# Layer 1 of a two-layer decoder trunk: output projection and feed-forward with one 512-column product per weight block

## The chip, the core and the metric

The kernel runs on one core of one Trainium2 chip. A core has TensorE (matrix products out of SBUF into PSUM banks of 512 fp32 columns; the trace calls its products PE and its weight loads PEld), VectorE (DVE), ScalarE (ACT), GpSimd (POOL) and SyncE (SP, which here issues nearly all DMAs). The metric is the device time of one execution in microseconds; the median of several runs is compared.

## What is computed

Two layers run over 272 tokens (16 meta tokens and 256 real ones) of width 1024. The part that the change touches is, per layer:

```python
merged = (gates[:, :, 0] * (out_a @ wb_a.T) + gates[:, :, 1] * (out_b @ wb_b.T)
          + gates[:, :, 2] * (out_c @ wb_c.T))
h_res = h_res + merged @ w_out[layer]
h2 = _rmsnorm(h_res, ln2_g[layer])
h_res = h_res + jnp.square(jax.nn.relu(h2 @ w_ff1[layer])) @ w_ff2[layer]
```

`w_out` is 1024x1024, `w_ff1` 1024x4096, `w_ff2` 4096x1024. Ahead of it in each layer stand one wide input projection and three attention branches. The meta tokens are dropped at the end, so layer 1 computes its queries, its output projection and its feed-forward for 256 tokens only, where layer 0 does so for all 272.

## The kernel before, in words

Activations lie transposed: features on the 128 partitions, tokens along the free dimension. `T` is 272; `q0` is 0 in layer 0 and 16 in layer 1, and `NQ = T - q0` is 272 and 256. All weights come from one packed array `wall`, in 2048-column DMAs into three `raw` buffers.

**Split precision.** Every large product is made of three fp32r matmuls. `split` (line 171) takes an fp32 tile apart: ScalarE casts it to fp32r (line 172, the high part `H`), VectorE subtracts that from the source (line 173, the low part `L`). `ws.next` does so with each weight block of 128x1024 (tiles `wh` and `wl`, three buffers each). `mm3` (lines 175 to 180) then issues three matmuls into one PSUM bank: weight high by activation high (line 178), weight low by activation high (line 179), weight high by activation low (line 180). Each loads its own 128x128 of weights and streams 272 or 256 columns of activations. The three together, for one 128x128 block of a weight, are called a block below.

**Stages of layer 1 that matter here.** *Output projection* (`wo`): 8 output tiles of 8 blocks each, from the merged branches in `mg`; the first two tiles run as a pair, interleaved, into banks of `ps_t`. `wo_done` adds the bank to the residual `xT` (line 982) and feeds the tile to the next norm: `NormIn.feed` makes its high and low part (lines 279 and 280) and the sum of squares (lines 293 and 294). *First feed-forward product* (`ff1`): 32 tiles of 8 blocks; the first two as a pair again, and right behind them the matmul of the norm's sum (line 300). `ff1_done` evicts: ScalarE's ReLU from PSUM to SBUF (line 1015), VectorE's square (line 1017), and a split into the pairs `fHL`, or `fH` and `fL`. *Second feed-forward product* (`ff2`): 8 tiles of 32 blocks; VectorE multiplies the bank by the squared norm factor (line 1038), adds it to `xT` (line 1039), and in layer 1 SyncE sends the tile out (line 1041). Apart from the two pairs, these stages use the pool `ps_acc` of two banks: a tile's bank is written again two tiles later, once it has been evicted. In all that makes 64 + 256 + 256 = 576 blocks, 72 times eight of them, and 1728 matmuls in layer 1.

**Order.** The order of the instructions on each engine is fixed when the program is built, by a scheduler that sorts ready instructions by their place in the program; each engine then works its queue strictly in that order, waiting on semaphores. In these stages the cast of a weight block waits until the tile that used its buffer three blocks earlier is finished.

**Other users of 512 columns.** `mla_prep` of each layer multiplies the latent by `ukv` in products of 512 columns (tiles `ps_uk` and `ps_vm`), with a weight load each; in the trace they are the only fp32r products of that width.

Of the kernel before, what the change touches and what calls it, by code (L numbers as in the profile page):

```python
# [79 lines left out]
def hybrid_trunk_kernel(ctx: ExitStack, tc: tile.TileContext, xin, wall, pcol, prow, consts, out):  # L80
# [100 lines left out]

    def minus_sums(ps, srcs):
# [82 lines left out]
    class NormIn:  # L265


        def __init__(self, l, gcol, off):
            self.l, self.g, self.off = l, gcol, off
            self.H = xg_p.tile([P, KD, T], F32R, tag="xgH", name="xgH")  # L270
            self.L = xg_p.tile([P, KD, T], F32R, tag="xgL", name="xgL")
# [35 lines left out]
    def gemm(w, h, c0, m=P, bank=0):  # L307

        pool, tag = ((ps_acc, "acc"), (ps_s, "s"), (ps_t, "t"))[bank]
        ps = pool.tile([P, 512], F32, tag=tag, name="acc")  # L310
        for kc in range(KD):
            mm3(ps[:m, : T - c0], blocks(w, kc, m), (h.H[:, kc, c0:], h.L[:, kc, c0:]), kc == 0, kc == KD - 1)
        return ps

    def proj(h, name, idx, c0, m=P, bank=0):
        return gemm(ws.next(name, idx), h, c0, m, bank)

    def gemm_pair(wl, h, c0):
        pss = s_banks(2)
        for kc in range(KD):  # L320
            for w, ps in zip(wl, pss):
                mm3(ps[:, : T - c0], blocks(w, kc), (h.H[:, kc, c0:], h.L[:, kc, c0:]), kc == 0, kc == KD - 1)
# [13 lines left out]
    def proj_group(h, names, c0s, banks):  # L336
        wl = [ws.next(n, i) for n, i in names]
        pss = banks(len(names))
        for kc in range(KD):
            for w, ps, c0 in zip(wl, pss, c0s):  # L340
                mm3(ps[:, : T - c0], blocks(w, kc), (h.H[:, kc, c0:], h.L[:, kc, c0:]), kc == 0, kc == KD - 1)
# [20 lines left out]
    def layer(l, h, rows):  # L362
# [591 lines left out]
        mg = [(v4(big("mgH", F32R)), v4(big("mgL", F32R))) for _ in range(2)]  # L954
        for j in range(KD):
# [17 lines left out]
            split(mg[j // 4][0][:, j % 4, :NQ], mg[j // 4][1][:, j % 4, :NQ], m[:, :NQ])  # L973
# [4 lines left out]
        def wo_rhs(k):  # L978
            return mg[k // 4][0][:, k % 4, :NQ], mg[k // 4][1][:, k % 4, :NQ]

        def wo_done(j, ps):
            V.tensor_tensor(out=xT[:, j, q0:], in0=xT[:, j, q0:], in1=ps[:, :NQ], op=ALU.add)
# [4 lines left out]
        for k in range(KD):  # L987
            for w, ps in zip(wl, pss):
                mm3(ps[:, :NQ], blocks(w, k), wo_rhs(k), k == 0, k == KD - 1)
        for j in range(2):  # L990
            wo_done(j, pss[j])
        for j in range(2, KD):
            w = ws.next("wo", j)
            ps = ps_acc.tile([P, 512], F32, tag="acc", name="acc")
            for k in range(KD):
                mm3(ps[:, :NQ], blocks(w, k), wo_rhs(k), k == 0, k == KD - 1)
# [5 lines left out]
        def act_pair(i):  # L1002

            g, r = divmod(i, 4)
            if g not in acts:
                if g < 3:
                    t = huge("fHL", F32R)
                    acts[g] = (v4(t), v4(t[:, 4 * T :]))
                else:
                    acts[g] = (v4(big("fH", F32R)), v4(big("fL", F32R)))  # L1010
            return acts[g][0][:, r, :NQ], acts[g][1][:, r, :NQ]

        def ff1_done(i, ps):
            r = row_p.tile([P, T], F32, tag="row", name="ffr")
            S.activation(r[:, :NQ], ps[:, :NQ], AF.Relu)  # L1015
            s = row_p.tile([P, T], F32, tag="row", name="ffs")
            V.tensor_tensor(out=s[:, :NQ], in0=r[:, :NQ], in1=r[:, :NQ], op=ALU.mult)  # L1017
# [175 lines left out]
```

## Time and profile before

| | |
|---|---|
| median of 3 runs | 977.07 us (976.43 to 977.22) |
| the profiled execution | 977.4 us |
| its span, from the first to the last instruction | 975.6 us |
| TensorE busy | 964.4 us (99%), 7614 matmuls |
| weight loads busy | 926.5 us (95%) |
| VectorE busy | 654.2 us (67%) |
| ScalarE busy | 588.7 us (60%) |
| granted TensorE clock | 1.000 |
| HBM read | 147.04 MB, 152 GB/s over the span |

Matmuls overlap in the records (a 256-column matmul's row is 0.28 us long, while the next one starts 0.12 us after it), so what TensorE really spends on one is read from start to start, not from the duration or the busy share. The granted clock of 1.000 is the upper of the two levels, 2.4 GHz. Some matmul records are missing, so counts out of the trace are a few below those of the program.

### The profile page before, as it was taken

What the parts mean: (1) busy time and instruction counts of PE and PEld (TensorE: products, weight loads), DVE (VectorE), ACT (ScalarE), POOL (GpSimd) and SP (SyncE); (2) the same over time, 40 slices, a digit from 0 to 9 for tenths busy, and PEclk for the clock granted to TensorE, in tenths of its full rate; (3) what the DMA queues carried; (4) which work ended last, traced back from release to release, by engine and by line L of the source; (5) the groups of instructions that cost most, each with busy time, mean ns of one, the idle gap of its engine ahead of it and who ended that gap; (6) DMA issues with size and microseconds to landing.
All of it is one profiled execution on the core that took longest, in us unless ns stands there. A gap on an engine that the chain in (4) does not pass through costs nothing.

```text
span 975.6 us, 18642 instructions
## 1 busy us (share of the span) xinstructions
PE 964.4 (99%) x7614; PEld 926.5 (95%) x7614; DVE 654.2 (67%) x1313; ACT 588.7 (60%) x1168; POOL 1.9 (0%) x7
## 2 busy tenths in 40 slices
PE   8999999999999999999999999999999999999998
PEld 7999999889999999999999998989899999999998
DVE  6975457686787666655557754487778876775553
ACT  6776777778635555544436777766795465554332
POOL 0000000000000000000000000000000000000000
PEclk9999999999999999999999999999999999999999
DMA  8432222325454445554544322324345555555551
GB/s 295 168 131 87 88 87 87 130 87 174 162 206 166 162 178 176 176 179 175 178 157 163 130 88 89 128 87 141 134 152 199 178 204 183 178 190 201 184 198 46
DMA packets 23958, 149.28 MB, mean 153 GB/s; under 512 B 2801, under 2 KB 4337, under 8 KB 8257
## 3 DMA queue, kind: packets, MB, share of 16 engines
q1 hardware_dynamic: 23760, 147.77, 43.6%
q8 instruction: 60, 0.98, 0.4%
q0 software_dynamic: 112, 0.33, 0.1%
q14 instruction: 26, 0.20, 0.1%
HBM read 147.04 MB, written 1.05 MB: 152 GB/s over the span
## 4 chain that ended last, share of the span: by engine, by line
PE 91%; DVE 4%; ACT 3%; DMA 1%; issue 0%; SPq 0%; DVEq 0%
PE acc L178 24%; PE acc L180 24%; PE acc L179 24%; PE ps_s L601 2%; PE accs L180 2%; PE accs L178 2%; PE accs L179 2%; PE ps_qkT L672 1%; ACT wh L172 1%; DVE wl L173 1%; PE ps_p L632 1%; PE ps_z L760 1%; PE acct L179 1%; PE acct L178 1%; PE acct L180 1%; PE pv_m L654 1%
## 5 line engine op out<-in xcount | busy, mean ns | idle before, releaser
L173 DVE TENSOR_TENSOR wl<-rawt,wh 128x1024 fp32r<-128x1024 f32 (+1 forms) x273 | 327.9, 1203 | 153.8 <-ACT wh L172 152.9
L172 ACT CAST wh<-rawt 128x1024 fp32r<-128x1024 f32 (+1 forms) x273 | 280.4, 1029 | 201.2 <-PE acc L180 177.2
L178 PE MATMUL acc<-xgH,wh 128*128 128x272 f32 (+2 forms) x1280 | 371.7, 290 | 1.0 <-DVE gate L892 0.9
L179 PE MATMUL acc<-xgH,wl 128*128 128x272 f32 (+2 forms) x1280 | 367.8, 287 | 1.2 <-DVE wl L173 1.2
L180 PE MATMUL acc<-xgL,wh 128*128 128x272 f32 (+2 forms) x1280 | 367.5, 287 | 0.0
L178 PEld LDWEIGHTS acc<-xgH,wh 128*128 128x128 f32 (+1 forms) x1280 | 240.0, 188 | 3.9 <-DVE gate L892 1.7
L179 PEld LDWEIGHTS acc<-xgH,wl 128*128 128x128 f32 (+1 forms) x1280 | 239.7, 187 | 2.9 <-DVE wl L173 1.7
L180 PEld LDWEIGHTS acc<-xgL,wh 128*128 128x128 f32 (+1 forms) x1280 | 240.0, 188 | 1.7 <-issue 1.3
L180 PE MATMUL acc<-fL,wh 128*128 128x272 f32 (+1 forms) x320 | 91.3, 285 | 0.0
L179 PE MATMUL acc<-fH,wl 128*128 128x272 f32 (+1 forms) x320 | 91.1, 285 | 0.0
L178 PE MATMUL acc<-fH,wh 128*128 128x272 f32 (+1 forms) x320 | 91.1, 285 | 0.0
L1015 ACT ACTIVATE ffr<-acc 128x272 f32<-128x272 f32 (+1 forms) x60 | 23.5, 391 | 73.5 <-PE acc L180 73.5
L180 PEld LDWEIGHTS acc<-fL,wh 128*128 128x128 f32 x320 | 60.4, 189 | 0.0
L178 PEld LDWEIGHTS acc<-fH,wh 128*128 128x128 f32 x320 | 60.4, 189 | 0.0
L179 PEld LDWEIGHTS acc<-fH,wl 128*128 128x128 f32 x320 | 60.2, 188 | 0.0
L180 PE MATMUL acc<-fHL,wh 128*128 128x272 f32 (+1 forms) x192 | 54.8, 285 | 0.0
L178 PE MATMUL acc<-fHL,wh 128*128 128x272 f32 (+1 forms) x192 | 54.7, 285 | 0.0
L179 PE MATMUL acc<-fHL,wl 128*128 128x272 f32 (+1 forms) x192 | 54.7, 285 | 0.0
L1017 DVE TENSOR_TENSOR ffs<-ffr 128x272 f32<-128x272 f32 (+1 forms) x64 | 27.8, 434 | 28.6 <-ACT ffr L1015 28.5
L180 PEld LDWEIGHTS acc<-fHL,wh 128*128 128x128 f32 x192 | 36.2, 189 | 0.0
L178 PEld LDWEIGHTS acc<-fHL,wh 128*128 128x128 f32 x192 | 36.2, 189 | 0.0
L179 PEld LDWEIGHTS acc<-fHL,wl 128*128 128x128 f32 x192 | 36.1, 188 | 0.0
(304 smaller groups left out, 1602.3 us busy)
## 6 DMA issues: line engine op xcount, KB each, us to landing
rawt<-wall SPq DMA_DIRECT2D x122, 1024.0 KB, 4.9
rawt<-wall SPq DMA_DIRECT2D x12, 768.0 KB, 4.2
rawt<-wall SPq DMA_DIRECT2D x4, 896.0 KB, 4.8
rawt<-wall SPq DMA_DIRECT2D x6, 256.0 KB, 7.1
xT<-xin SPq DMA_DIRECT2D x4, 272.0 KB, 6.7
rawt<-wall SPq DMA_DIRECT2D x2, 512.0 KB, 6.3
out<-xT SPq DMA_DIRECT2D x8, 128.0 KB, 3.9
rawt<-wall SPq DMA_DIRECT2D x1, 640.0 KB, 3.8
```

What stands on the lines that cost most here:

```text
L172: S.copy(dH, src)
L173: V.tensor_tensor(out=dL, in0=src, in1=f(dH), op=ALU.subtract)
L178: PE.matmul(ps, lhsT=aH, rhs=bH, start=start, stop=False)
L179: PE.matmul(ps, lhsT=aL, rhs=bH, start=False, stop=False)
L180: PE.matmul(ps, lhsT=aH, rhs=bL, start=False, stop=stop)
L601: PE.matmul(ps[:, po : po + nk], lhsT=qa[:, qo - q0 : qo - q0 + P], rhs=ka[:, k0 : k0 + nk], start=True, stop=True)
L632: PE.transpose(p1[:, P * i : P * i + P], a, ident)
L654: PE.matmul(pv[:, o : o + n], lhsT=vs[w], rhs=pt[:, 256 * w : 256 * w + n], start=False, stop=w == 1)
L672: PE.transpose(ps[:96, o : o + n], src[c][:n, hd, :], ident[:n, :n])
L760: PE.matmul(z[:, :W], lhsT=upper, rhs=s[:, :W], stop=False, **kw)
L1015: S.activation(r[:, :NQ], ps[:, :NQ], AF.Relu)
L1017: V.tensor_tensor(out=s[:, :NQ], in0=r[:, :NQ], in1=r[:, :NQ], op=ALU.mult)
```

## The change

In layer 1 (`NQ == SEQ`) the products of `wo`, `ff1` and `ff2` take a new form. The high and the low part of an activation now lie side by side in one tile (`xgHL`, `mgHL`, `fHL`: for each feature block first the high and then the low columns, 272 apart). One matmul multiplies the weight's high part by both, as one moving operand of two runs of 256 columns, into 512 columns of a bank; a second multiplies the weight's low part by the activation's high part into the first 256. So a bank holds two halves, and whoever evicts it sums them: `joined` copies the second half to SBUF (ScalarE) and adds the first (VectorE). `ff1_done` calls it in place of the ReLU, and does ReLU and square in one VectorE instruction; the eviction of `ff2` calls it ahead of its multiplication; `wo_done` adds both halves to `xT`, one after the other. Layer 0, and all products ahead of `wo` in layer 1, keep their three matmuls; for them only the layout of the tiles changes.

```diff
--- before.py
+++ after.py
@@ -179,6 +179,25 @@
         PE.matmul(ps, lhsT=aL, rhs=bH, start=False, stop=False)
         PE.matmul(ps, lhsT=aH, rhs=bL, start=False, stop=stop)
 
+    def dense(ps, a, HL, start, stop, side=False):
+
+
+        aH, aL = a
+        n = HL.shape[2]
+        if not side:
+            mm3(ps[:, :n], a, (HL[:, 0], HL[:, 1]), start, stop)
+        else:
+            PE.matmul(ps[:, : 2 * n], lhsT=aH, rhs=HL, start=start, stop=False)
+            PE.matmul(ps[:, :n], lhsT=aL, rhs=HL[:, 0], start=False, stop=stop)
+
+    def joined(out, ps, n):
+
+        if n > SEQ:
+            return ps[:, :n]
+        S.copy(out, ps[:, n : 2 * n])
+        V.tensor_tensor(out=out, in0=out, in1=ps[:, :n], op=ALU.add)
+        return out
+
     def minus_sums(ps, srcs):
 
         for i, src in enumerate(srcs):
@@ -267,8 +286,8 @@
 
         def __init__(self, l, gcol, off):
             self.l, self.g, self.off = l, gcol, off
-            self.H = xg_p.tile([P, KD, T], F32R, tag="xgH", name="xgH")
-            self.L = xg_p.tile([P, KD, T], F32R, tag="xgL", name="xgL")
+            self.HL = xg_p.tile([P, KD, 2, T], F32R, tag="xgHL", name="xgHL")
+            self.H, self.L = self.HL[:, :, 0], self.HL[:, :, 1]
             self.ss = st_p.tile([P, T], F32, tag="ss", name="ss", bufs=1)
             self.n = 0
 
@@ -304,22 +323,22 @@
     def blocks(w, kc, m=P):
         return w[0][:, kc * m : kc * m + m], w[1][:, kc * m : kc * m + m]
 
-    def gemm(w, h, c0, m=P, bank=0):
+    def gemm(w, h, c0, m=P, bank=0, side=False):
 
         pool, tag = ((ps_acc, "acc"), (ps_s, "s"), (ps_t, "t"))[bank]
         ps = pool.tile([P, 512], F32, tag=tag, name="acc")
         for kc in range(KD):
-            mm3(ps[:m, : T - c0], blocks(w, kc, m), (h.H[:, kc, c0:], h.L[:, kc, c0:]), kc == 0, kc == KD - 1)
+            dense(ps[:m], blocks(w, kc, m), h.HL[:, kc, :, c0:], kc == 0, kc == KD - 1, side)
         return ps
 
-    def proj(h, name, idx, c0, m=P, bank=0):
-        return gemm(ws.next(name, idx), h, c0, m, bank)
+    def proj(h, name, idx, c0, m=P, bank=0, side=False):
+        return gemm(ws.next(name, idx), h, c0, m, bank, side)
 
     def gemm_pair(wl, h, c0):
         pss = s_banks(2)
         for kc in range(KD):
             for w, ps in zip(wl, pss):
-                mm3(ps[:, : T - c0], blocks(w, kc), (h.H[:, kc, c0:], h.L[:, kc, c0:]), kc == 0, kc == KD - 1)
+                dense(ps, blocks(w, kc), h.HL[:, kc, :, c0:], kc == 0, kc == KD - 1)
         return pss
 
     def spread_bank(i):
@@ -333,12 +352,12 @@
     def s_banks(n):
         return [ps_s.tile([P, 512], F32, tag="s", name="accs") for _ in range(n)]
 
-    def proj_group(h, names, c0s, banks):
+    def proj_group(h, names, c0s, banks, side=False):
         wl = [ws.next(n, i) for n, i in names]
         pss = banks(len(names))
         for kc in range(KD):
             for w, ps, c0 in zip(wl, pss, c0s):
-                mm3(ps[:, : T - c0], blocks(w, kc), (h.H[:, kc, c0:], h.L[:, kc, c0:]), kc == 0, kc == KD - 1)
+                dense(ps, blocks(w, kc), h.HL[:, kc, :, c0:], kc == 0, kc == KD - 1, side)
         return pss
 
     def big(name, dt=F32):
@@ -951,7 +970,7 @@
                     tc.add_manual_dep(i, u.name, NOSYNC, reason="table order")
                 sig.append(i)
 
-        mg = [(v4(big("mgH", F32R)), v4(big("mgL", F32R))) for _ in range(2)]
+        mg = [big("mgHL", F32R).rearrange("p (a i t) -> p a i t", a=2, i=2) for _ in range(4)]
         for j in range(KD):
             wab = ws.next("wbab", j)
             sigmoids(j)
@@ -970,30 +989,31 @@
                     t = row_p.tile([P, T], F32, tag="row", name="mrt")
                     V.tensor_tensor(out=t[:, :NQ], in0=ps[:, :NQ], in1=g, op=ALU.mult)
                     V.tensor_tensor(out=m[:, :NQ], in0=m[:, :NQ], in1=t[:, :NQ], op=ALU.add)
-            split(mg[j // 4][0][:, j % 4, :NQ], mg[j // 4][1][:, j % 4, :NQ], m[:, :NQ])
+            split(mg[j // 2][:, j % 2, 0, :NQ], mg[j // 2][:, j % 2, 1, :NQ], m[:, :NQ])
 
         load_log_exp(sig)
         n2 = NormIn(l, PC_LN2, q0)
 
         def wo_rhs(k):
-            return mg[k // 4][0][:, k % 4, :NQ], mg[k // 4][1][:, k % 4, :NQ]
+            return mg[k // 2][:, k % 2, :, :NQ]
 
         def wo_done(j, ps):
-            V.tensor_tensor(out=xT[:, j, q0:], in0=xT[:, j, q0:], in1=ps[:, :NQ], op=ALU.add)
+            for a in (0, NQ)[: 2 if NQ == SEQ else 1]:
+                V.tensor_tensor(out=xT[:, j, q0:], in0=xT[:, j, q0:], in1=ps[:, a : a + NQ], op=ALU.add)
             n2.feed(j)
 
         wl = [ws.next("wo", j) for j in range(2)]
         pss = t_banks(2)
         for k in range(KD):
             for w, ps in zip(wl, pss):
-                mm3(ps[:, :NQ], blocks(w, k), wo_rhs(k), k == 0, k == KD - 1)
+                dense(ps, blocks(w, k), wo_rhs(k), k == 0, k == KD - 1, NQ == SEQ)
         for j in range(2):
             wo_done(j, pss[j])
         for j in range(2, KD):
             w = ws.next("wo", j)
             ps = ps_acc.tile([P, 512], F32, tag="acc", name="acc")
             for k in range(KD):
-                mm3(ps[:, :NQ], blocks(w, k), wo_rhs(k), k == 0, k == KD - 1)
+                dense(ps, blocks(w, k), wo_rhs(k), k == 0, k == KD - 1, NQ == SEQ)
             wo_done(j, ps)
 
 
@@ -1001,30 +1021,37 @@
 
         def act_pair(i):
 
-            g, r = divmod(i, 4)
+            g, r = divmod(i, 2)
             if g not in acts:
-                if g < 3:
-                    t = huge("fHL", F32R)
-                    acts[g] = (v4(t), v4(t[:, 4 * T :]))
+                if i < 12:
+                    t = huge("fHL", F32R)[:, : 8 * T].rearrange("p (g a i t) -> p g a i t", g=2, a=2, i=2)
+                    acts[g], acts[g + 1] = t[:, 0], t[:, 1]
                 else:
-                    acts[g] = (v4(big("fH", F32R)), v4(big("fL", F32R)))
-            return acts[g][0][:, r, :NQ], acts[g][1][:, r, :NQ]
+                    acts[g] = big("fHL", F32R).rearrange("p (a i t) -> p a i t", a=2, i=2)
+            return acts[g][:, r, :, :NQ]
 
         def ff1_done(i, ps):
             r = row_p.tile([P, T], F32, tag="row", name="ffr")
-            S.activation(r[:, :NQ], ps[:, :NQ], AF.Relu)
             s = row_p.tile([P, T], F32, tag="row", name="ffs")
-            V.tensor_tensor(out=s[:, :NQ], in0=r[:, :NQ], in1=r[:, :NQ], op=ALU.mult)
-            split(*act_pair(i), s[:, :NQ])
-
-        pss = proj_group(n2, [("ff1", i) for i in range(2)], [q0] * 2, t_banks)
+            if NQ > SEQ:
+                S.activation(r[:, :NQ], ps[:, :NQ], AF.Relu)
+                V.tensor_tensor(out=s[:, :NQ], in0=r[:, :NQ], in1=r[:, :NQ], op=ALU.mult)
+            else:
+                joined(r[:, :NQ], ps, NQ)
+                V.scalar_tensor_tensor(
+                    out=s[:, :NQ], in0=r[:, :NQ], scalar=0.0, in1=r[:, :NQ], op0=ALU.max, op1=ALU.mult
+                )
+            t = act_pair(i)
+            split(t[:, 0], t[:, 1], s[:, :NQ])
+
+        pss = proj_group(n2, [("ff1", i) for i in range(2)], [q0] * 2, t_banks, NQ == SEQ)
         for i in range(2):
             ff1_done(i, pss[i])
         n2.finish()
         r2 = n2.rstd
         S.activation(r2[:, q0:], r2[:, q0:], AF.Square)
         for i in range(2, 32):
-            ff1_done(i, proj(n2, "ff1", i, q0))
+            ff1_done(i, proj(n2, "ff1", i, q0, side=NQ == SEQ))
 
         nxt = None if last else NormIn(l + 1, PC_LN1, 0)
         for j in range(KD):
@@ -1033,9 +1060,9 @@
                 w = ws.next("ff2", 4 * j + i)
                 for k in range(8):
                     kk = 8 * i + k
-                    mm3(ps[:, :NQ], blocks(w, k), act_pair(kk), kk == 0, kk == 31)
+                    dense(ps, blocks(w, k), act_pair(kk), kk == 0, kk == 31, NQ == SEQ)
             t = row_p.tile([P, T], F32, tag="row", name="fft")
-            V.tensor_tensor(out=t[:, :NQ], in0=ps[:, :NQ], in1=r2[:, q0:], op=ALU.mult)
+            V.tensor_tensor(out=t[:, :NQ], in0=joined(t[:, :NQ], ps, NQ), in1=r2[:, q0:], op=ALU.mult)
             V.tensor_tensor(out=xT[:, j, q0:], in0=xT[:, j, q0:], in1=t[:, :NQ], op=ALU.add)
             if last:
                 nc.sync.dma_start(out[j], xT[:, j, q0:])
```

## Rows read from the trace of the kernel before

**Rows 1.** The page: TensorE's busy time, its granted clock, and the chain's lines

```profile
PE 964.4 (99%) x7614; PEld 926.5 (95%) x7614; DVE 654.2 (67%) x1313; ACT 588.7 (60%) x1168; POOL 1.9 (0%) x7
...
PEclk9999999999999999999999999999999999999999
...
PE 91%; DVE 4%; ACT 3%; DMA 1%; issue 0%; SPq 0%; DVEq 0%
```

**Rows 2.** Stretches, TensorE alone: length, busy (matmuls), granted clock, DMA share, GB/s

```profile
772.60:795.20 22.60, 22.60 (x194) 1.00 0.53 187
795.20:881.30 86.10, 86.10 (x729) 1.00 0.52 184
881.30:972.00 90.70, 90.65 (x767) 1.00 0.47 162
```

**Rows 3.** Waits from 770 us on: waiting for: total us, times, longest

```profile
DVE wl L173 <- ACT wh L172: 54.2, 65, 1.6
ACT wh L172 <- PE acc L180: 53.2, 31, 1.8
ACT ffr L1015 <- PE acc L180: 34.4, 29, 1.3
```

**Rows 4.** Timeline of ScalarE in ff1: start, us, instruction [idle before <-releaser]

```profile
849.92 0.39 ACT L1015 ACTIVATE ffr<-acc 128x256 f32<-128x256 f32 x1 [1.22 <-PE acc L180]
850.20 1.04 ACT L172 CAST wh<-rawt 128x1024 fp32r<-128x1024 f32 x1
851.14 0.41 ACT L172 CAST fH<-ffs 128x256 fp32r<-128x256 f32 x1
...
861.28 0.39 ACT L1015 ACTIVATE ffr<-acc 128x256 f32<-128x256 f32 x1 [1.21 <-PE acc L180]
```

**Rows 5.** Timeline of VectorE in ff1, the same tiles

```profile
850.34 0.43 DVE L1017 TENSOR_TENSOR ffs<-ffr 128x256 f32<-128x256 f32 x1 [0.34 <-ACT ffr L1015]
851.28 1.23 DVE L173 TENSOR_TENSOR wl<-rawt,wh 128x1024 fp32r<-128x1024 f32 x1 [0.51 <-ACT wh L172]
852.42 0.42 DVE L173 TENSOR_TENSOR fL<-ffs,fH 128x256 fp32r<-128x256 f32 x1
```

**Rows 6.** Timeline of TensorE, 256 columns: a quick run in the attention stage

```profile
513.29 0.28 PE L178 MATMUL accs<-xgH,wh 128*128 128x256 f32 x1
...
513.63 0.28 PE L178 MATMUL accs<-xgH,wh 128*128 128x256 f32 x1
```

**Rows 7.** Timeline of TensorE, 512 columns: layer 0's `mla_prep`, then layer 1's

```profile
34.63 0.40 PE L179 MATMUL ps_uk<-wh,latHL 128*128 128x512 f32 x1
...
36.02 0.40 PE L179 MATMUL ps_uk<-wh,latHL 128*128 128x512 f32 x1
```

**Rows 8.** The same view, layer 1's `mla_prep`

```profile
531.25 0.39 PE L179 MATMUL ps_uk<-wh,latHL 128*128 128x512 f32 x1
...
532.87 0.39 PE L180 MATMUL ps_uk<-wl,latHL 128*128 128x512 f32 x1
```

**Rows 9.** Timeline of VectorE at the end of the span

```profile
971.99 0.42 DVE L1038 TENSOR_TENSOR fft<-acc,rstd 128x256 f32<-128x256 f32 x1 [6.21 <-PE acc L180]
972.45 0.43 DVE L1039 TENSOR_TENSOR xT<-xT,fft 128x256 f32<-128x256 f32 x1
```

**Rows 10.** Timeline of VectorE in wo: a tile's eviction, and the last tile's square sum

```profile
787.18 0.41 DVE L982 TENSOR_TENSOR xT<-xT,acc 128x256 f32<-128x256 f32 x1
788.16 1.23 DVE L173 TENSOR_TENSOR wl<-rawt,wh 128x1024 fp32r<-128x1024 f32 x1 [0.57 <-ACT wh L172]
...
792.53 0.42 DVE L294 TENSOR_TENSOR ss<-ss,sq 128x256 f32<-128x256 f32 x1
```

**Rows 11.** Timeline of VectorE behind the pair of ff1: its idle times there

```profile
796.47 1.23 DVE L173 TENSOR_TENSOR wl<-rawt,wh 128x1024 fp32r<-128x1024 f32 x1 [0.51 <-ACT wh L172]
...
800.10 1.23 DVE L173 TENSOR_TENSOR wl<-rawt,wh 128x1024 fp32r<-128x1024 f32 x1 [0.26 <-ACT wh L172]
...
802.94 1.22 DVE L173 TENSOR_TENSOR wl<-rawt,wh 128x1024 fp32r<-128x1024 f32 x1 [0.27 <-ACT wh L172]
```

## The prediction, made before the changed kernel was built or timed

> **What bounds the kernel now.** I read the page first, for the engine that is never idle: TensorE is busy for 99% of the span at the full granted clock, and 91% of the chain of work that ended last lies on it [rows 1]. An average can hide a stage with another limit, so I then cut the changed stages out: `wo`, `ff1` and `ff2` of layer 1 fill 772.6 to 972.0 us, and in each of them TensorE is busy from end to end [rows 2]. The waits of that stretch say the same from the other side: all the long ones are ScalarE waiting for TensorE to finish a tile, or VectorE waiting for ScalarE [rows 3]; no wait of TensorE is among them. So these stages last as long as TensorE takes for their blocks, and the other engines matter only if the change makes one of them late. Last I read the period of a tile from the ReLUs: from 849.92 to 861.28 us lie four tiles, 2.84 us for each, or 355 ns per block of three matmuls, 118.3 ns from start to start [rows 4]. The stretch of `ff2` gives the same: 90.7 us for its 256 blocks, 354 ns each [rows 2].
>
> **What the change does to a block.** The columns that TensorE streams stay the same: 512 and 256 in place of three times 256. What goes is one matmul with its weight load per block. So the gain is whatever a matmul costs beyond its columns, and that I read from how the time grows with the width. At 256 columns it is 118.3 ns [rows 4]. At 512 the trace has the products of `mla_prep`: six of them from 34.63 to 36.02 us make 231.7 ns each [rows 7], seven from 531.25 to 532.87 us make 231.4 [rows 8]. I take 231.5. A block then costs 231.5 + 118.3 = 349.8 ns in place of 355.0: 5.2 ns less. Times 576 blocks this is 3.0 us.
>
> This price has two unknowns. The 512-column rows stream one run of columns, while the new operand has two runs of 256, a step apart; no fp32r product of the trace streams 512 columns so. If a run pays as a matmul of its own does, 512 columns cost 2 x 118.3 = 236.6 ns [rows 4] and the gain of a block is 0. On the other side, 118.3 ns is no floor: in the attention stage three successive 256-column matmuls take 0.34 us, 113.3 ns each [rows 6]. What makes the others 5 ns slower the trace doesn't tell. If the new order always ran at the quick pace, a block would cost 3 x 113.3 = 340 ns, 15 ns less, 8.7 us in all. I take the middle value, since the rows of 512 columns are nearest to the new matmul in width, type and weight load, and since 72 groups of eight blocks in a row run at the slow pace today.
>
> **What is added at the evictions, and what hides it.** In `ff1` ScalarE's ReLU becomes its copy of the second half, of the same size; I price it at the ReLU's 0.39 us [rows 4]. VectorE gets one more addition per tile, 0.42 us by the square's row, and the square becomes an instruction with a maximum in it; I take the same 0.42 and add 0.06 for doubt. VectorE's starts follow each other 0.08 us sooner than durations suggest (1.14 us from `wl` at 851.28 to `fL` at 852.42 [rows 5]), so the addition occupies about 0.40 us. Per tile VectorE has today 0.34 + 0.51 = 0.85 us of idle time [rows 5]. So 0.46 us fits, and what is left, 0.85 - 0.46 - 0.04 (the shorter tile) = 0.35 us, is small. The place fits as well: the addition starts where the square starts now, at 850.34; the square follows it by 0.46 us, as one dependent VectorE instruction follows another at the end of the span [rows 9], and is done at 851.22 us; the next `wl` starts at 851.28 [rows 5]. The split of the result waits for the weight's cast on ScalarE, until 851.14 [rows 4], so it moves by some 0.1 us. Queued behind the addition on VectorE are that `wl` and the `fL` of the same tile. Who waits for `wl` is the matmul three tiles after the one whose buffer was freed, two tiles later (5.6 us), so it may be late by microseconds. The bank is freed by the addition, some 0.45 us later than by the ReLU now (850.31), at 850.76; the tile that uses it next starts a tile after, at 852.7. Cost on TensorE: nothing. If the cover were gone, each tile would pay what its bank came late (rival 3).
>
> Behind the pair of `ff1` VectorE is fuller: from 795.5 to 803 us it is idle three times, for 0.51, 0.26 and 0.27 us [rows 11], and five tiles add 0.46 us each. About 1.3 us of backlog builds there and goes at 0.35 us a tile; the bank's slack of 1.9 us and the weights' of 5.6 take it. In `wo` the second addition of a tile starts 0.46 us after the first (787.18 to 787.64) and ends at 788.06, before `wl` at 788.16 [rows 10]: nothing again. For the last tile of `wo` the square sum stands at 792.53 [rows 10], and TensorE reaches the matmul that reads it only at the end of `ff1`'s pair, about 795.3; 0.46 us are hidden. In `ff2` VectorE is idle for 6.21 us ahead of the last eviction [rows 9]; seven of eight evictions cost nothing.
>
> **What lies on the path.** The last eviction does. Today the multiplication starts at 971.99 us, 0.46 us later the addition, and the tile is sent [rows 9]. Now a ScalarE copy and a VectorE addition come ahead of it. From the ReLU to the VectorE instruction that needs it the trace has 0.42 us (849.92 to 850.34 [rows 4, 5]); the addition takes another 0.46 to its dependent [rows 9]. Sum: 0.88 us at the end of the span. No DMA is added or moved: the weights' traffic is the same, at half of the DMA engines' time [rows 2], and 1.5% more of it per time is far from their limit. The new layouts of the tiles move no work in layer 0; I cost them at nothing, with 0.3 us either way for another order of small instructions.
>
> **The sum.** 3.0 - 0.88 = 2.1 us less than the profiled execution's 977.4 us (its span of 975.6 us and 1.8 us around it), 975.3 us. The median of the runs is 0.33 us below the profiled execution, so against it the time is 974.9 us.
>
> **Rivals.** *1. The fixed part of a matmul is smaller than I take, or the second run eats it.* For it: the price of the two-run operand is on no row. Against it: 231.5 is less than twice 118.3 by 5.1 ns, in both layers [rows 7, 8]. With a gain of 0 ns a block the tail alone remains: 977.07 + 0.88 = 977.95 us. The Trainium skill has a rule that speaks against the change here: the page "TensorE: Matmul & The Clock Gate", section "Back-to-back issue gap", gives an isolated warm matmul N/2.4 + 2.5 ns, so one matmul less would save 2.5 ns of a block, 1.4 us of the whole, and the time would be an estimated 976.5 us, within 0.2% too. By that rule 256 and 512 columns take 109.2 and 215.8 ns; the trace, with a weight load for each, has 118.3 and 231.5 and so agrees in neither.
>
> *2. The quick pace.* With one weight load less in each block, TensorE may run as it does in the short stretch of [rows 6]. For it: that pace exists, with the same kind of operands. Against it: the 512-column rows aren't quick (226.6 would be twice 113.3). Then a block gains 15 ns, and the time is 977.07 - 8.7 + 0.88 = 969.3 us; half of that effect gives about 973.
>
> *3. A bank comes late, and the kernel is slower.* The order on VectorE is set when the program is built. If it puts the tile's addition behind the next `wl` and `fL`, it starts 0.34 us after 852.42, at 852.76, and ends at 853.18; the bank is wanted at 852.7, half a microsecond earlier. The tile after next starts late by that; the one behind it then finds its bank free, so every second of 30 tiles pays: 15 x 0.5 = 7.5 us, 974.9 + 7.5 = 982.4 us. It decides from the point where the addition ends more than one tile (2.8 us) after the bank's last matmul. For it: the idle time shrinks from 0.85 to 0.35 us a tile. Against it: the eviction's first step is put ahead of the next weight in all tiles now [rows 4, 5], and the addition is ready 0.9 us before `wl` is.
>
> **How the numbers follow.** A measurement of this kernel can tell about 0.2%, 2 us, from no change; 0.2% faster is 975.1 us, so my forecast lies at that bound. The forecast's own case (3 to 8 ns a block, 976.2 to 973.3 us) gets 0.54, of which 0.31 lies below the bound; rival 1 gets 0.15, rival 2 with all between 8 and 15 ns 0.17, rival 3 0.14. Faster by over 0.2%: 0.31 + 0.17 = 0.48. Within 0.2%: 0.23 + 0.15 = 0.38. Slower: 0.14. The range leaves out the far part of rivals 2 and 3: 971.5 to 979.0 us. The forecast's own range is 973.3 to 976.2.
>
> **What would show it.** In the profile of the changed kernel: the period of the `ff1` copies at 2.80 us (2.84 now); 512-column matmuls of `wo`, `ff1` and `ff2` starting 231 to 232 ns before the next one, and 256-column ones 118; no wait of TensorE for VectorE or ScalarE from `wo` on; VectorE's first addition at 0.42 us behind the copy, and ahead of `wl`; the last DMA issued about 0.9 us further behind the last matmul. Wrong would be: 236 or more for the 512 columns (rival 1); 113 for the 256 behind them (rival 2); matmuls that wait for the joining addition (rival 3); or a change in layer 0, where I expect none.

## The result: slower by 1.1%

The changed kernel takes 987.81 us (median of 4 runs, 986.56 to 987.99) against 977.14 us before (976.43 to 977.55). The ratio is 1.0108, with a 95% interval of 1.0097 to 1.0120. The forecast was 974.9 us in a range of 971.5 to 979.0.

Where it went is seen by cutting the traces at the first matmul of `wo`, at the norm's matmul behind `ff1`'s pair, and at the first and the last matmul of `ff2`. The changed kernel's profiled execution has a span of 986.2 us, and `layout` and `best` are two kernels of the experiments below (us).

| stretch | before | after | `layout` | `best` |
|---|---|---|---|---|
| start to layer 1's `wo` | 767.02 | 765.76 | 765.55 | 765.76 |
| `wo` and `ff1`'s pair | 28.48 | 29.21 | 28.51 | 28.19 |
| `ff1` behind its pair | 85.41 | 96.81 | 85.42 | 84.41 |
| `ff2`, to its last matmul | 90.77 | 89.59 | 90.35 | 89.59 |
| from there to the end | 3.97 | 4.82 | 3.96 | 3.98 |

The loss is in `ff1`: 11.4 us. `ff2`, with the same new matmuls, gains 1.2 us; the tail costs 0.85, `wo` with the pair 0.7, and the start is 1.3 us shorter, 0.8 of it by the new layout (below), while the rest differs between profiles of one and the same stretch. From the page of the changed kernel:

```profile
PE 967.3 (98%) x7038; PEld 899.1 (91%) x7038; DVE 670.4 (68%) x1361; ACT 591.3 (60%) x1176; POOL 1.9 (0%) x7
...
PEclk9999999999999999999999999999999989999999
...
PE 84%; DVE 7%; ACT 5%; issue 2%; DMA 1%; SPq 0%; DVEq 0%; ACTq 0%
```

576 matmuls are gone, as intended. But the chain leaves TensorE for 16% of the span where it was 9% [rows 1], and one slice of the clock's row is below 9. The busy share of 98% hides it: a stall of 3.5 us is 0.4% of the span. The waits of TensorE from 760 us on (waiting for: total us, times, longest) name what it waited for; before the change this answer was empty:

```profile
PE acc L190 <- DVE ffr L198: 4.6, 7, 3.5
PE acc L190 <- DVE xT L1002: 0.6, 1, 0.6
```

Line 190 is the new 512-column matmul, line 198 the joining addition of `ff1`, line 1002 that of `wo`. Seven waits for `ff1`'s are counted there; 15 more appear on the weight loads (`PEld acc L190 <- DVE ffr L198: 6.6, 15, 0.5`, in the same query for all engines). So the banks came late, which was rival 3. Its place is seen in the middle of `ff1`, on ScalarE:

```profile
833.86 1.05 ACT L172 CAST wh<-rawt 128x1024 fp32r<-128x1024 f32 x1 [1.19 <-PE acc L190]
834.81 0.40 ACT L172 CAST fHL<-ffs 128x256 fp32r<-128x256 f32 x1
835.12 0.36 ACT L197 COPY ffr<-acc 128x256 f32<-128x256 f32 x1
837.11 1.05 ACT L172 CAST wh<-rawt 128x1024 fp32r<-128x1024 f32 x1 [1.62 <-issue]
838.06 0.40 ACT L172 CAST fHL<-ffs 128x256 fp32r<-128x256 f32 x1
838.36 0.36 ACT L197 COPY ffr<-acc 128x256 f32<-128x256 f32 x1
```

and on VectorE in the same tiles:

```profile
834.94 1.23 DVE L173 TENSOR_TENSOR wl<-rawt,wh 128x1024 fp32r<-128x1024 f32 x1 [0.47 <-ACT wh L172]
836.08 0.42 DVE L173 TENSOR_TENSOR fHL<-ffs,fHL 128x256 fp32r<-128x256 f32 x1
836.42 0.41 DVE L198 TENSOR_TENSOR ffr<-ffr,acc 128x256 f32<-128x256 f32 x1
836.87 0.43 DVE L1041 SCALAR_TENSOR_TENSOR ffs<-ffr 128x256 f32<-128x256 f32 x1
838.19 1.23 DVE L173 TENSOR_TENSOR wl<-rawt,wh 128x1024 fp32r<-128x1024 f32 x1 [0.89 <-ACT wh L172]
```

Before, ScalarE's order was ReLU, cast of a weight, cast of the result [rows 4], and VectorE's was square, `wl`, `fL` [rows 5]. Now the weight's cast comes first and the copy of the bank last, with the cast of the *previous* tile's result between them. On VectorE `wl` and the previous `fHL` stand ahead of the joining addition. The tile whose copy starts at 835.12 ended at 833.72 (0.12 us behind the start of its last matmul); its bank is free at 836.83, 3.1 us later, and a tile lasts 2.8. Every second tile waits, and two tiles together take 6.06 us (from 839.67 to 845.73 on the joining additions).

The large stall stands at the start of the stage, behind the pair. The copies of the tiles 2 and 3 (counted from 0), which ended at 798.0 and 800.8 us, wait in ScalarE's queue behind a weight's cast, the cast of an earlier result and the three instructions of the norm (`rs_y`, `rs_w`):

```profile
800.90 1.04 ACT L172 CAST wh<-rawt 128x1024 fp32r<-128x1024 f32 x1 [1.16 <-issue]
801.86 0.40 ACT L172 CAST fHL<-ffs 128x256 fp32r<-128x256 f32 x1
802.16 0.47 ACT L121 ACTIVATE rs_y<-ps_ss,eps 128x256 f32<-128x256 f32 x1
802.66 0.42 ACT L121 ACTIVATE rs_y<-rs_y 128x256 f32<-128x256 f32 x1
803.11 0.42 ACT L220 ACTIVATE rs_w<-rs_y 128x256 f32<-128x256 f32 x1
803.43 0.63 ACT L197 COPY ffr<-acc 128x256 f32<-128x256 f32 x2
```

and TensorE stands until 804.46 us. Before the first of these casts ScalarE had itself been idle for 1.16 us, with tile 2 long ended: it works its queue in the order given. What follows is seen by stretches, TensorE alone (length, busy, granted clock, DMA share, GB/s):

```profile
800.90:804.40 3.50, 0.04 (x1) 0.87 0.85 290
804.40:809.80 5.40, 5.34 (x17) 0.50 0.03 11
```

The clock fell to its lower level during the stall, 1.2 GHz, and a whole tile ran at it: 5.25 us, from 804.46 to 809.71, where others take 2.8.

So `ff1` lost 3.7 us to the stall (6.48 us from the start of tile 3 to that of tile 4, 2.81 in `best`), 2.4 to the clock and 6.3 to the waits of every second tile (82.1 us for its last 27 tiles, 75.8 in `best`), and gained 1.0.

### The profile page after: what moved, and what is told of

It is laid out like the page before. It is cut to its first block, busy times and chain, and to the rows that moved or that the text cites. A ratio compares the mean times of both kernels' runs of the same rounds, so it can differ in the third digit from the quotient of the medians.

```text
span 986.2 us, 17547 instructions
## 1 busy us (share of the span) xinstructions
PE 967.3 (98%) x7038; PEld 899.1 (91%) x7038; DVE 670.4 (68%) x1361; ACT 591.3 (60%) x1176; POOL 1.9 (0%) x7
## 4 chain that ended last, share of the span: by engine, by line
PE 84%; DVE 7%; ACT 5%; issue 2%; DMA 1%; SPq 0%; DVEq 0%; ACTq 0%
PE acc L178 17%; PE acc L180 17%; PE acc L179 17%; PE acc L190 9%; PE acc L191 4%; ACT wh L172 3%; DVE wl L173 3%; PE ps_s L620 2%; PE accs L180 2%; PE accs L179 2%; PE accs L178 2%; PE ps_qkT L691 1%; PE ps_p L651 1%; PE ps_z L779 1%; PE pv_m L673 1%
## 5 line engine op out<-in xcount | busy, mean ns | idle before, releaser
L178 PE MATMUL acc<-xgHL,wh 128*128 128x272 f32 (+1 forms) x1040 | 303.5, 292 | 1.0 <-DVE gate L911 0.9
L179 PE MATMUL acc<-xgHL,wl 128*128 128x272 f32 (+1 forms) x1040 | 299.9, 288 | 0.9 <-DVE wl L173 0.9
L180 PE MATMUL acc<-xgHL,wh 128*128 128x272 f32 (+1 forms) x1040 | 299.3, 288 | 0.0
L178 PEld LDWEIGHTS acc<-xgHL,wh 128*128 128x128 f32 x1040 | 194.3, 187 | 3.8 <-DVE gate L911 1.7
L179 PEld LDWEIGHTS acc<-xgHL,wl 128*128 128x128 f32 x1040 | 194.5, 187 | 2.6 <-DVE wl L173 1.5
L180 PEld LDWEIGHTS acc<-xgHL,wh 128*128 128x128 f32 x1040 | 194.5, 187 | 1.7 <-issue 1.3
L190 PE MATMUL acc<-xgHL,wh 128*128 128x512 f32 x240 | 89.4, 413 | 5.4 <-DVE ffr L198 4.6
L190 PE MATMUL acc<-fHL,wh 128*128 128x512 f32 x256 | 89.8, 393 | 0.1
L180 PE MATMUL acc<-fHL,wh 128*128 128x272 f32 x256 | 74.0, 289 | 0.0
L178 PE MATMUL acc<-fHL,wh 128*128 128x272 f32 x256 | 73.6, 288 | 0.0
L179 PE MATMUL acc<-fHL,wl 128*128 128x272 f32 x256 | 73.5, 287 | 0.0
L191 PE MATMUL acc<-fHL,wl 128*128 128x256 f32 x256 | 72.1, 282 | 0.0
L190 PEld LDWEIGHTS acc<-xgHL,wh 128*128 128x128 f32 x240 | 46.4, 193 | 20.8 <-DVE ffr L198 6.2
L190 PEld LDWEIGHTS acc<-fHL,wh 128*128 128x128 f32 x256 | 48.0, 187 | 11.5 <-DVE ffr L198 0.4
L180 PEld LDWEIGHTS acc<-fHL,wh 128*128 128x128 f32 x256 | 48.2, 188 | 0.0
L178 PEld LDWEIGHTS acc<-fHL,wh 128*128 128x128 f32 x256 | 48.1, 188 | 0.0
L191 PEld LDWEIGHTS acc<-xgHL,wl 128*128 128x128 f32 x240 | 46.5, 194 | 0.0
```

The lines of the kernel that those rows point to most:

```text
L178: PE.matmul(ps, lhsT=aH, rhs=bH, start=start, stop=False)
L179: PE.matmul(ps, lhsT=aL, rhs=bH, start=False, stop=False)
L180: PE.matmul(ps, lhsT=aH, rhs=bL, start=False, stop=stop)
L190: PE.matmul(ps[:, : 2 * n], lhsT=aH, rhs=HL, start=start, stop=False)
L191: PE.matmul(ps[:, :n], lhsT=aL, rhs=HL[:, 0], start=False, stop=stop)
```

## The experiments

Three theories stood against each other. *A, the order:* in the new form the last matmul of a tile reads the weight's low part, so the high part's buffer is free one matmul before the bank is. The next weight's cast, which waits for that buffer, is ready first and is placed ahead of the copy. *B, the load:* the longer eviction is simply too much. *C, the matmul:* the operand of two runs costs what it was to save. That the cast now waits for another matmul than the copy is on a row of the changed kernel's waits from 760 us on (the copy waits for line 191, as the last one does here):

```profile
ACT wh L172 <- PE acc L190: 70.4, 44, 3.5
...
ACT fft L197 <- PE acc L191: 7.5, 1, 7.5
```

In the kernel before, both the cast and the ReLU wait for line 180 [rows 3].

**`swap`: the two matmuls of a tile's last block exchanged.**

```diff
+            if stop:
+                PE.matmul(ps[:, :n], lhsT=aL, rhs=HL[:, 0], start=False, stop=False)
-            PE.matmul(ps[:, : 2 * n], lhsT=aH, rhs=HL, start=start, stop=False)
-            PE.matmul(ps[:, :n], lhsT=aL, rhs=HL[:, 0], start=False, stop=stop)
+            PE.matmul(ps[:, : 2 * n], lhsT=aH, rhs=HL, start=start, stop=stop)
+            if not stop:
+                PE.matmul(ps[:, :n], lhsT=aL, rhs=HL[:, 0], start=False, stop=False)
```

> Edit: in the changed kernel, the last block of each tile of layer 1's three stages issues its 256-column matmul (weight low) first and its 512-column matmul (weight high) last; all other blocks as they are. Theory of the order (A): in the changed kernel the last matmul of a tile no longer reads the weight's high part, so that buffer is free one matmul (0.12 us) before the bank is, the next cast of a weight is put ahead of the copy of the bank on ScalarE, and the joining addition ends some 3 us after the tile; with the two matmuls exchanged both come free together, the copy goes first, and the time is 974.5 to 976.5 us (my prediction's sum), with no wait of TensorE for the joining addition in ff1. Theory of the load (B): one more VectorE and a longer eviction per tile are too much for two banks whatever the order: 986 to 989 us as in the changed kernel. Theory of the matmul (C): the two-run operand is what costs: 986 to 989 us.

Measured: 976.25 us, 0.9993 (0.9983 to 1.0003) of the 976.65 us of before on the same chip. Exchanging two instructions per tile, with the same work, takes the whole loss away. ScalarE in the middle of `ff1`:

```profile
840.57 0.37 ACT L200 COPY ffr<-acc 128x256 f32<-128x256 f32 x1 [1.08 <-PE acc L192]
840.84 1.05 ACT L172 CAST wh<-rawt 128x1024 fp32r<-128x1024 f32 x1
841.89 0.41 ACT L172 CAST fHL<-ffs 128x256 fp32r<-128x256 f32 x1
```

and VectorE:

```profile
840.98 0.42 DVE L201 TENSOR_TENSOR ffr<-ffr,acc 128x256 f32<-128x256 f32 x1 [0.30 <-ACT ffr L200]
841.43 0.42 DVE L1044 SCALAR_TENSOR_TENSOR ffs<-ffr 128x256 f32<-128x256 f32 x1
841.93 1.23 DVE L173 TENSOR_TENSOR wl<-rawt,wh 128x1024 fp32r<-128x1024 f32 x1
843.07 0.42 DVE L173 TENSOR_TENSOR fHL<-ffs,fHL 128x256 fp32r<-128x256 f32 x1
```

The copy is first again, the addition stands ahead of `wl`, and VectorE still idles 0.30 us a tile: the place and the 0.35 us that the prediction had worked out. Two waits of TensorE stay, 0.9 us in `wo` and 0.6 behind the pair; with the longer tail they eat what the matmuls gain, so it is no faster than before. B and C fall as causes of the loss.

**`pin`: the changed kernel's own matmuls, the order prescribed.** If only the exchange had been tried, something else about it could have helped. In `split`, `a` and `b` are the cast and the subtraction; `pins` holds the copy and the joining addition of each tile.

```diff
+        if pin_now:
+            for i, u in zip((a, b), pin_now[0]):
+                tc.add_manual_dep(i.ins, u.ins.name, NOSYNC, reason="copy first")
...
+            if NQ == SEQ and i >= 3:
+                pin_now[:] = [pins[i - 3]]
+            w = ws.next("ff1", i)
+            pin_now[:] = []
-            ff1_done(i, proj(n2, "ff1", i, q0, side=NQ == SEQ))
+            ff1_done(i, gemm(w, n2, q0, side=NQ == SEQ))
```

> Edit: the changed kernel with its own order of matmuls, but in layer 1's ff1 the cast of a weight block and the subtraction behind it must come, in the order of their engines, after the copy and the joining addition of the tile that frees their buffer (an order without a wait). A (the order is the cause): the stall behind the pair, the half clock and the waits of every second tile go; what stays is wo's wait of 0.65 us and the tail: 975.5 to 977 us. If the exchange of the two matmuls in the run before had helped by something other than the order: 984 us or more.

Measured: 976.18 us, 0.9993 (0.9984 to 1.0002) of 976.9. TensorE's waits from 760 us on are 0.6 us in `wo` and 0.4 in `ff1`. No instruction differs from the changed kernel; the order alone is worth some 11 us.

**`half`: the new matmuls with the short eviction, which leaves the second half of the bank out of the result.**

```diff
-            for a in (0, NQ)[: 2 if NQ == SEQ else 1]:
+            for a in (0,):
...
-        if n > SEQ:
+        if True:
             return ps[:, :n]
...
-            if NQ > SEQ:
+            if True:
                 S.activation(r[:, :NQ], ps[:, :NQ], AF.Relu)
```

> Edit: the changed kernel's matmuls with the evictions of before, which read the first half of the bank alone; the products of the weight's high part with the activation's low part are left out of the result. A: the cast is still put ahead of the ReLU, but the ReLU frees the bank 1.4 us after the tile, in time; no tail: 977.1 - 3.0 = 974.1, from 973 to 975.5 us. B: the same, 973 to 975.5. C: the matmuls cost what they cost in the changed kernel: 984 us or more.

Measured: 973.47 us, 0.9967 (0.9956 to 0.9978) of 976.65. Here too the cast comes first:

```profile
841.68 1.05 ACT L172 CAST wh<-rawt 128x1024 fp32r<-128x1024 f32 x1 [1.17 <-PE acc L190]
842.63 0.40 ACT L172 CAST fHL<-ffs 128x256 fp32r<-128x256 f32 x1
842.94 0.38 ACT L1037 ACTIVATE ffr<-acc 128x256 f32<-128x256 f32 x1
```

yet no tile in the middle of `ff1` waits, since the ReLU itself frees the bank, 1.6 us after the cast's start. So the 11 us need both: `swap` has the longer eviction without the order, `half` the order without the longer eviction. What the longer eviction costs in the good order is the next run.

**`three_mm`: the new evictions with three matmuls.**

```diff
-            PE.matmul(ps[:, : 2 * n], lhsT=aH, rhs=HL, start=start, stop=False)
-            PE.matmul(ps[:, :n], lhsT=aL, rhs=HL[:, 0], start=False, stop=stop)
+            PE.matmul(ps[:, :n], lhsT=aH, rhs=HL[:, 0], start=start, stop=False)
+            PE.matmul(ps[:, :n], lhsT=aL, rhs=HL[:, 0], start=False, stop=False)
+            PE.matmul(ps[:, n : 2 * n], lhsT=aH, rhs=HL[:, 1], start=False, stop=stop)
```

> Edit: the changed kernel's evictions with the three matmuls of before: weight high by activation high and weight low by activation high into the first half of the bank, weight high by activation low into the second. A: the last matmul reads the weight's high part again, so copy and cast keep the order of the kernel before; only the tail of 0.88 us is paid, and no matmul is saved: 977 to 979 us. B: the evictions are those of the changed kernel and the matmuls those of before: 3 us more than the changed kernel, 989 to 991 us, or at least above 984. C: 977 to 978 us.

Measured: 978.67 us, 1.0019 (1.0010 to 1.0029) of 976.65. The evictions alone cost 2 us in a good order: by the trace 1.1 in `wo`, 0.9 in `ff1` and the tail's 0.85, less what the layout gives (below). The sum lies in the range, but the expectation had the tail's share alone. With the weight's high part last, the copy is first.

**`banks`: five banks for `ff1`.**

```diff
+            w, ps = ws.next("ff1", i), spread_bank(i)
+            for kc in range(KD):
+                dense(ps, blocks(w, kc), n2.HL[:, kc, :, q0:], kc == 0, kc == KD - 1, True)
+            ff1_done(i, ps)
```

> Edit: the changed kernel, but the tiles 2 to 31 of layer 1's ff1 take their banks from five (two of ps_acc, three of ps_s) in place of two. A: the bank may come 3 us late without anyone waiting, so the 3.5 us stall behind the pair, the stretch at half clock after it and the waits of every second tile go, though the cast stays ahead of the copy: 975 to 977 us. B: if VectorE or ScalarE were overloaded, more banks would only put the wait off: above 983 us. C: 986 to 989 us.

Measured: 979.60 us, 1.0030 (1.0019 to 1.0041) of 976.65. Most of the loss goes, but the time lies 2.6 us above the range. With the order left as it was, the evictions run late all through the stage, nobody waits for them, and the first tile of `ff2`, which still has two banks to choose from, pays at the end:

```profile
PE acc L190 <- DVE ffr L198: 3.1, 1, 3.1
PE acc L190 <- DVE xT L1002: 0.6, 1, 0.6
```

Its stretches there (as above) show the clock's fall a second time:

```profile
878.70:881.90 3.20, 0.16 (x2) 0.97 0.74 261
881.90:885.20 3.30, 3.26 (x10) 0.52 0.15 65
885.20:900.00 14.80, 14.80 (x87) 1.00 0.42 152
```

**`wo_ff2`: `ff1` in its old form.**

```diff
-        pss = proj_group(n2, [("ff1", i) for i in range(2)], [q0] * 2, t_banks, NQ == SEQ)
+        pss = proj_group(n2, [("ff1", i) for i in range(2)], [q0] * 2, t_banks)
...
-            ff1_done(i, proj(n2, "ff1", i, q0, side=NQ == SEQ))
+            ff1_done(i, proj(n2, "ff1", i, q0))
```

> Edit: the changed kernel with ff1 in its old form (three matmuls, ReLU from PSUM); wo and ff2 in the new one. A: everything that was lost sat in ff1. ff2 gains 1.2 us, wo gains 0.3 and loses its wait of 0.65, the tail costs 0.85: no net change from these, 976.4 to 977 us; if the layout gives 0.8 us in layer 0, 975.6 to 976.4. If wo or ff2 had a share in the loss: 979 or more.

Measured: 976.21 us, 0.9995 (0.9986 to 1.0005) of 976.9: with the old `ff1` nothing is lost, and nothing is won.

**`layout`: the new tiles alone.** The edit takes back all of the new matmuls and evictions (`side` is never set, `joined` returns the bank); the tiles with high and low part side by side stay.

> Edit: the changed kernel's tiles (high and low part side by side) with the matmuls and evictions of before everywhere. In the profiles so far layer 0's feed-forward, which the change gives only the new layout, is some 0.8 us shorter than before (from the first to the last norm matmul around it), and this would be the layout's or chance. If the layout does it: 975.6 to 976.2 us against 976.65 of before. If it is chance of one profile: 976.4 to 976.9. My prediction had nothing for the layout, +-0.3 us.

Measured: 975.66 us, 0.9988 (0.9979 to 0.9997) of 976.9. The layout, which I had costed at nothing, is worth 1.2 us. In its trace layer 0's feed-forward, from one norm matmul to the next, takes 190.73 us where it took 191.54, in all profiles with the new tiles alike, and layer 1's `ff2` 90.35 where it took 90.77. The numbers of matmuls are the same; a block of three takes some 1.6 ns less (0.81 us over 512 blocks, 0.42 over 256).

**`fill` and `fill8`: TensorE kept busy through the stall.** Both put matmuls that nothing reads between the fourth and the fifth tile of the changed kernel's `ff1`, 14 of them or 8:

```diff
+            if NQ == SEQ and i == 4:
+                fill = ps_t.tile([P, 512], F32, tag="t", name="fill")
+                for _ in range(14):
+                    PE.matmul(fill[:, :SEQ], lhsT=ones, rhs=xT[:, 0, q0:], start=True, stop=True)
```

> Edit: the changed kernel with 14 more matmuls of 256 columns in fp32 (215 ns each by the norm's matmul), some 3.0 us, on TensorE alone, into a bank that nothing reads, between the fourth and the fifth tile of layer 1's ff1, where TensorE stands for 3.5 us. Order and work of the other engines stay. If the half clock that follows there (8 blocks at 640 in place of 350 ns) comes of TensorE's standing still, it stays away and the stall itself remains: 987.8 - 2.5 = 985.3 us, from 984.5 to 986. If the half clock has another cause, it stays: 987.5 to 988.5 us; if the matmuls only push the work behind them, later still.

Measured: 987.38 us, 1.0108 (1.0090 to 1.0126) of 976.9. The clock stayed full, but each of these matmuls took 0.42 us (the trace has two records for one, 0.21 us apart), where I had reckoned 0.215; 14 of them ended at 806.15 us where the bank was ready some 2 us earlier, and that ate the gain. My arithmetic, not the idea, had failed, so I took 8.

> Edit: the run before with 8 filling matmuls in place of 14. There each took two passes of 215 ns, so that the 14 lasted 5.9 us and overran the 3.5 us wait by about 2 us, which ate the gain of the full clock; 8 last 3.4 us and fit. If TensorE's standing still brings the half clock: the clock stays full, and tile 4 to tile 5 takes 2.8 to 3.0 us in place of 5.25; 987.8 - 2.3 = 985.5 us, from 984.5 to 986.3. If the backlog of the evictions sets the pace all the same, the gain is lost again in later waits: 986.5 to 988.

Measured: 984.57 us, 1.0075 (1.0058 to 1.0092) of 977.19; the changed kernel was 987.81 beside 977.14, so 3.2 us less (2.6 of it in `ff1` by the traces). Its stretches behind the stall:

```profile
800.40:803.80 3.40, 3.40 (x18) 1.00 0.82 287
803.80:806.80 3.00, 2.94 (x16) 1.00 0.17 71
```

The tile behind the stall takes 2.88 us (804.29 to 807.17) in place of 5.25. More work on TensorE made the kernel faster: the half clock came of its standing still, and cost that tile 2.4 us.

**`best`: the exchange, five banks everywhere, the old form for the last tile.**

```diff
-            ps = ps_acc.tile([P, 512], F32, tag="acc", name="acc")
+            ps = spread_bank(j + 2) if last else ps_acc.tile([P, 512], F32, tag="acc", name="acc")
+            two = last and j < KD - 1
...
-                    dense(ps, blocks(w, k), act_pair(kk), kk == 0, kk == 31, NQ == SEQ)
+                    dense(ps, blocks(w, k), act_pair(kk), kk == 0, kk == 31, two)
```

(with the edits of `swap` and `banks`, and `spread_bank(j + 1)` in `wo`).

> Edit: the changed kernel with the two matmuls of each tile's last block exchanged, wo, ff1 and ff2 of layer 1 taking their banks from five in place of two, and the last tile of ff2 in the old form, so that nothing is joined at the end. A: the waits of 0.9 us in wo and 0.65 us behind the pair, which the exchanged order still had, go, and the tail's 0.85 us: 976.25 - 0.9 - 0.65 - 0.7 = 974.0 us, from 973.3 to 975. If those waits come back at another place: 975 to 976.5.

Measured: 973.35 us, 0.9963 (0.9949 to 0.9976) of 976.9: faster than both kernels, and TensorE has no wait from 760 us on. Its end shows the tail as it was before the change [rows 9], multiplication and addition and nothing ahead of them:

```profile
968.27 0.42 DVE L1075 TENSOR_TENSOR fft<-accs,rstd 128x256 f32<-128x256 f32 x1 [6.17 <-PE accs L180]
968.73 0.43 DVE L1076 TENSOR_TENSOR xT<-xT,fft 128x256 f32<-128x256 f32 x1
```

Of its 3.6 us the layout alone has 1.2; the rest, 2.3, fits what the new matmuls gain (2.1 us by the traces, below).

## Why the prediction was wrong, point by point

**The step that failed** is the one that costed the evictions of `ff1` at nothing. It took ScalarE's and VectorE's order from the kernel before ("the eviction's first step is put ahead of the next weight in all tiles now") and fitted the addition into the idle time there. The fit was right: in `swap` the addition starts where it should, and 0.30 us a tile are left. But the order was not a given. It stood because both ScalarE instructions waited for the same matmul, the one that reads the weight's high part last [rows 3], and the diff itself turns that around: its last matmul is the one with the weight's low part. I read the diff for what it adds to the engines, and not for which buffer each matmul is the last to read.

**Rival 3 was the mechanism**, with its place on VectorE, its point of decision (the addition ends more than a tile behind the bank's last matmul: 3.1 against 2.8 us) and its price in the steady part: two tiles of 2.80 us and a wait of 0.5 make 6.10, measured 6.06. That the price fits so well is partly luck. The rival took the bank to be wanted at 852.7 us, but in the trace of the kernel before the tile that writes it next starts at 852.50:

```profile
849.54 0.28 PE L180 MATMUL acc<-xgL,wh 128*128 128x256 f32 x1
...
852.50 0.28 PE L178 MATMUL acc<-xgH,wh 128*128 128x256 f32 x1
```

By its own times the wait would have been 0.7 us; but the addition came to end 3.1 us behind its tile, where the rival had 3.5 (849.66 to 853.18). It had a chance of 0.14, it gave no reason for the order to change and named VectorE's queue alone, not ScalarE's, where the copy falls behind the cast, and it left out the start of the stage. There I had found a backlog of 1.3 us and a slack of 1.9, again in the old order; in the new one the copies of two tiles stood behind the norm's instructions, and 3.7 us of stall and 2.4 us of half clock came on top. 982.4 and 6.1 make 988.5 us; measured were 987.8.

**The matmul's price was about right.** From the changed kernel's `ff2`, 512 columns and 256:

```profile
977.64 0.39 PE L190 MATMUL acc<-fHL,wh 128*128 128x512 f32 x1
...
981.14 0.39 PE L190 MATMUL acc<-fHL,wh 128*128 128x512 f32 x1
```

Ten blocks in 3.50 us are 350 ns each, against 349.8 predicted; the second run of the operand costs nothing to speak of, so a gain of nothing (rival 1) and one of 15 ns (rival 2) both fall. But part of the gain isn't the merged matmul's. Measured against `layout`, which has the same tiles, a block of `ff2` gains 3.0 ns (353 to 350) and one of `ff1` 4.2 (85.42 to 84.41 us over 240 blocks), in all about 2.1 us of the 3.0 predicted, or 3.6 ns a block. The estimate of 2.5 ns for a matmul saved, from the isolated gap that the Trainium skill gives ("TensorE: Matmul & The Clock Gate", "Back-to-back issue gap"), lies nearer to this mean than my 5.2, though its gaps for one matmul, 109.2 and 215.8 ns, are still below all rows here.

**The tail** was right: 0.85 us, 0.88 predicted. The chain at the end of the changed kernel:

```profile
981.37 0.28 PE L191 MATMUL acc<-fHL,wl 128*128 128x256 f32 x1
981.68 0.37 ACT L197 COPY fft<-acc 128x256 f32<-128x256 f32 x1 [7.46 <-PE acc L191]
982.09 0.42 DVE L198 TENSOR_TENSOR fft<-fft,acc 128x256 f32<-128x256 f32 x1 [6.61 <-ACT fft L197]
982.55 0.42 DVE L1065 TENSOR_TENSOR fft<-fft,rstd 128x256 f32<-128x256 f32 x1
983.01 0.42 DVE L1066 TENSOR_TENSOR xT<-xT,fft 128x256 f32<-128x256 f32 x1
```

**`wo`** was costed at nothing and lost 0.7 us net. The prediction had a tile's second addition follow the first by 0.46 us, ahead of `wl`. In the changed kernel a `wl` stands between the two, here those of the first tile behind the pair:

```profile
774.96 0.41 DVE L1002 TENSOR_TENSOR xT<-xT,acc 128x256 f32<-128x256 f32 x1
775.29 1.22 DVE L173 TENSOR_TENSOR wl<-rawt,wh 128x1024 fp32r<-128x1024 f32 x1
776.42 0.41 DVE L1002 TENSOR_TENSOR xT<-xT,acc 128x256 f32<-128x256 f32 x1
```

VectorE, which also has the pair's four additions to do there, falls behind, and one bank comes 0.6 to 0.9 us late in every kernel with the new eviction and two banks in `wo`. This too was an order read from the kernel before, and the exchange doesn't cure it: in `swap` the wait is 0.9 us.

**The layout** was costed at nothing, +-0.3 us; it gives 1.2.

## What to carry to other kernels

When a change reorders or drops the last reader of a buffer, ask which instructions wait for that buffer and which for the result: where they waited for the same event before, their order on a strictly ordered engine is about to be decided anew, and idle time read from the old order no longer vouches for anything. Ending a tile with the matmul that frees both at once kept most of a longer eviction hidden here (`swap`), and more banks in all three stages the rest (`best`); more banks in one stage alone moved the stall to the next (`banks`). Judge a stage by its start and its hand-over to the next one as well as by its steady period: that is where a backlog was paid here, and a stall of TensorE cost more than its own length: 2.4 us of clock on top of 3.7 in the changed kernel, 1.4 on top of 3.1 in `banks` (its `ff2` takes 91.0 us, that of the changed kernel 89.6).

## What the runs showed of the hardware

- TensorE's clock fell to half, a granted 0.50, while it stood still for 3.5 us (the changed kernel) and 3.1 us (`banks`), and stayed at 1.00 through stands of 0.4 to 0.9 us (`swap`, `pin`, `three_mm`). Matmuls that nothing reads kept it at 1.00 (`fill8`), for a gain of 3.2 us on the whole.
- A 512-column fp32r matmul whose operand is two runs of 256 columns starts the next one after 231 ns or so, as one with a single run does [rows 7, 8].
- With the activations' high and low part side by side, 272 columns apart, a block of the same three matmuls took 1.6 ns less: 0.8 us on layer 0's feed-forward, 0.4 on layer 1's `ff2`, and nothing on layer 1's `ff1` (85.42 and 85.41 us). Whether the parts share a tile isn't what counts. In the kernel before, blocks of layer 1's `ff2` take 355, 352, 356 and 357 ns from start to start, in turn through each four features; so do the 12 features whose parts lay in one tile even then, 1088 columns apart, and so do the 20 whose parts lay in two. With `layout` 353 and 354 ns take turns, and the weights lie as before. So a matmul's time goes with the place of its moving operand in SBUF; what about the place does it is open.
